# One core, two chained transformer blocks: a k-step of the modulation product as four quarters of 256 columns on TensorE's four column groups, in place of two halves of 512 on two of them

## The chip, the core and the metric

The kernel runs on one core of a Trainium2 chip. The metric is the device time of one execution in microseconds (us); of several runs the median is taken. All data is float32.

## What is computed

A first block of two layers (gated linear attention and latent attention side by side, then an MLP) is followed by a second block of one layer (dilated attention and a long convolution). Each of the three layers is steered by a modulation, a product of one conditioning row with a wide matrix, whose result is cut into shifts, scales and gates:

```python
cond = jax.nn.silu(c)
for l in range(DEPTH):                                   # two layers
    mod = (cond @ w_ada[l] + b_ada[l])[:, None, :]       # 1024 -> 6 x 1024
    shift_a, scale_a, gate_a, shift_f, scale_f, gate_f = jnp.split(mod, N_MOD, axis=-1)
    h = rms_norm(x) * (1.0 + scale_a) + shift_a
    mix = hybrid_mixer(h, ...)
    x = x + gate_a * mix
    h = rms_norm(x) * (1.0 + scale_f) + shift_f
    x = x + gate_f * (jnp.square(jax.nn.relu(h @ w_mlp_up[l])) @ w_mlp_down[l])
...
mod = (c @ w_ada + b_ada)[:, None, :]                    # second block: 1024 -> 3 x 1024
shift, scale, gate = jnp.split(mod, 3, axis=-1)
```

## The kernel before

There are 15 sections of 1,024 modulation values: six for each layer of the first block, three for the second block. `modulation` (L258) computes one section in eight k-steps, one for each 128 rows of the matrix. A k-step loads a tile `wada` of 128 rows by 1,024 columns (512 KB, L270, from SP's queue) and multiplies it with the conditioning column of these rows, which is repeated 32 times (`crep`, L301), so that the product is 32 equal rows. That uses 32 of the 128 columns of TensorE's array, so the product can be put on one of four column groups of 32 (`tile_position`), and products on different groups can run side by side. Two halves `g` of 512 columns stand on two groups, and the k-steps with even and odd `k` use different pairs:

```python
for g in range(2):
    q = 32 * (2 * (k % 2) + g)
    self.mm(ps[q : q + 32], cond[:, k, :], w[:, g * 512 : g * 512 + 512], k < 2, k >= NF - 2, tile_position=(0, q))
yield
```

So the four groups of the accumulator `modps` hold two partial sums of each half, which are added at the end of the section. VectorE copies `modps` into `modrow` (L276). Then the row has to be turned into a column layout (`mod`, 128 by 8). The two sections that the program starts with (`first`) do it on TensorE with products by `pick` (L283 to L286). The other 13 write the row to memory, read it back in column order (L288 to L291, ACT's queue) and add the two partial sums and the bias on VectorE (L292, L293).

The two first sections run in the program's first 50 us. The other 13 run as filling work inside the latent attention (MLA) of the two layers: six sections (48 k-steps) in layer 0, seven (56 k-steps) in layer 1. In `layer1` (L493) the function `spread` asks the generator `fill` for the next k-step twice in each step `n` of the attention loop, in proportion. The final order on each engine is set by a scheduler when the program is built; in the fill a k-step mostly stands alone between products of the attention: scores (`s_ps`), transposes (`tp`), values (`pv`), preparations of the next head (`n_ps`, `mv_ps`, `ms`). A `wada` tile of the fill has three buffers, and `modps` one.

A float32 product such as `modps` shows as two records (two passes) in the trace; the attention's products are of a type that shows as one.

Of the kernel before, what the change touches and what calls it, by code (L numbers as in the profile page):

```python
# [9 lines left out]
F32 = mybir.dt.float32  # L10
# [9 lines left out]
NF = D // 128  # L20
# [141 lines left out]
class Kernel:  # L162
    def __init__(self, tc, ins, consts, out):
        self.tc = tc
        self.nc = tc.nc
        self.i = ins
        self.k = consts
        self.out = out
        self.load = [0.0, 0.0]
# [88 lines left out]
    def modulation(self, p, name, secs, bufs=2, first=False):  # L258

        nc = self.nc  # L260
        cond, w_ada, b_ada = self.ada[name]
        for s in secs:

            if first:
                ps = self.PS.tile([128, 512], F32, name="modps", tag="big", bufs=2, padded_shape=[128, 1024])
            else:
                ps = self.PS.tile([128, 512], F32, name="modps", tag="mod", bufs=1)
            for k in range(NF):
                w = p.tile([128, 1024], F32, name="wada", tag="wada", bufs=bufs + (0 if first else 1))
                nc.sync.dma_start(w, w_ada[k * 128 : (k + 1) * 128, s * 1024 : s * 1024 + 1024])  # L270
                for g in range(2):
                    q = 32 * (2 * (k % 2) + g)
                    self.mm(ps[q : q + 32], cond[:, k, :], w[:, g * 512 : g * 512 + 512], k < 2, k >= NF - 2, tile_position=(0, q))
                yield
            row = p.tile([128, 512], F32, name="modrow", tag="modrow", bufs=1)
            nc.vector.tensor_copy(row, ps)  # L276
            out = self.base.tile([128, NF], F32, name=f"mod_{name}{s}")
            col = self.base.tile([128, 3, NF], F32, name="modcol", tag="modcol", bufs=2)
            nc.scalar.dma_start(col[:, 0], b_ada[s * 1024 : s * 1024 + 1024].rearrange("(j p) -> p j", p=128))
            self.mods[name, s] = out  # L280
            if first:

                cps = self.PS.tile([128, 4, 2], F32, name="modcol_ps", tag="sm", bufs=2, padded_shape=[128, 4, 128])  # L283
                for j in range(4):
                    self.mm(cps[:, j], row[:, j * 128 : j * 128 + 128], self.pick, True, True)
                nc.vector.tensor_add(out.rearrange("p (g j) -> p j g", g=2), cps, col[:, 0].rearrange("p (g j) -> p j g", g=2))  # L286
                continue
            rows = self.DR.tile([4, 512], F32, name=f"modrow_{name}{s}")  # L288
            for q in range(4):
                nc.scalar.dma_start(rows[q].unsqueeze(0), row[32 * q : 32 * q + 1, :])  # L290
            nc.scalar.dma_start(col[:, 1:3], rows.rearrange("(b g) (j p) -> p b (g j)", b=2, p=128))  # L291
            nc.vector.tensor_add(out, col[:, 1], col[:, 2])  # L292
            nc.vector.tensor_add(out, out, col[:, 0])  # L293

    def cond_cols(self, c, silu, name):
        nc = self.nc
# [67 lines left out]
    def consts(self):  # L364
        nc, C, k = self.nc, self.C, self.k
        self.ident = C.tile([128, 128], F32, name="ident")
        nc.sync.dma_start(self.ident, k["ident"])
        self.ones_d = C.tile([128, 128], F32, name="ones_d")
        nc.gpsimd.memset(self.ones_d, -1.0 / 1024)

        self.pick = C.tile([128, 2], F32, name="pick")
        nc.gpsimd.memset(self.pick, 0.0)
        for q in range(4):
            nc.gpsimd.memset(self.pick[32 * q : 32 * q + 1, q % 2 : q % 2 + 1], 1.0)
        self.ones_n = C.tile([128, 128], F32, name="ones_n")
        nc.gpsimd.memset(self.ones_n, -1.0 / 128)
        self.ones_q = C.tile([128, 128], F32, name="ones_q")
        nc.gpsimd.memset(self.ones_q, -1.0 / 256)
        self.ones_r = C.tile([128, 128], F32, name="ones_r")
        nc.sync.dma_start(self.ones_r, k["blockones"])  # L380
        self.eps = C.tile([128, 1], F32, name="eps")
        nc.gpsimd.memset(self.eps, EPS)
# [1600 lines left out]
def trace(tc, ins, consts, out):  # L1983
    Kernel(tc, ins, consts, out).build()
# [21 lines left out]
```

## Time and profile before

| | us |
|---|---|
| three runs | 4498.74, 4505.05, 4512.79 |
| median | 4505.05 |
| the profiled execution | 4509.59 |
| its span in the trace | 4507.8 |
| TensorE matmul busy (PE) | 4159.8 (92%) |
| VectorE (DVE), ScalarE (ACT), GpSimd (POOL) busy | 2098.6, 1492.0, 1483.5 |
| mean granted TensorE clock | 0.961 of full speed |

The span is the time between the first and the last instruction of the profiled execution. PE is the row of matmuls and PEld that of weight loads, which run beside them. Matmuls are pipelined and their ends are modelled, so the time that one costs is read from the starts of its neighbours, not from its length. Timeline rows give start and length in us, then engine, line, operation, output<-inputs, shape and count.

### The profile page before, as it was taken

To read this page: it belongs to the slowest core of one execution; us is meant where nothing else is said; L and a number is where in the kernel's file an instruction comes from. 1 tells how busy PE (TensorE), PEld (TensorE's weight loads), DVE (VectorE), ACT (ScalarE), POOL (GpSimd) and SP (SyncE) were. 2 spreads that over 40 slices of the span, in tenths; PEclk is the share of its full clock that TensorE was granted. 3 is DMA by queue.
4 is the path that set the end of the run, shared out by engine and by line. 5 is a ranking of instruction groups with operands and counts; after the bars stand their busy time and mean duration, and the time that the engine had idled before them with its cause. 6 is when DMAs were issued, how large, how long until landed. Compare 5 with 4: busy or idle time off the path is not lost. (4 is left out here: it accounts for less than half of the span.)

```text
span 4507.8 us, 52345 instructions
## 1 busy us (share of the span) xinstructions
PE 4159.8 (92%) x19660; PEld 3217.8 (71%) x19660; DVE 2098.6 (47%) x3804; ACT 1492.0 (33%) x2824; POOL 1483.5 (33%) x1349
## 2 busy tenths in 40 slices
PE   6999888999999899988999999899999999887998
PEld 3775666888887585566788888667777767766777
DVE  6326575323335516576433333653322434577545
ACT  5435345121212524444312211332224444222222
POOL 3322355333332422155433333222230111355342
PEclk8999899999999999989999999999999999998999
DMA  6145434131111126543211111244453232554563
GB/s 193 57 140 146 150 109 126 43 110 47 52 47 52 42 84 197 156 135 117 76 51 48 47 47 43 93 121 115 112 141 89 85 86 61 178 157 152 167 196 112
DMA packets 579696, 471.25 MB, mean 105 GB/s; under 512 B 210728, under 2 KB 473930, under 8 KB 579314
## 3 DMA queue, kind: packets, MB, share of 16 engines
q1 hardware_dynamic: 375514, 367.43, 26.7%
q10 hardware_dynamic: 203192, 92.74, 7.3%
q0 software_dynamic: 736, 7.73, 0.5%
q8 instruction: 155, 2.54, 0.2%
q14 instruction: 99, 0.81, 0.1%
HBM read 364.22 MB, written 107.52 MB: 105 GB/s over the span
## 5 line engine op out<-in xcount | busy, mean ns | idle before, releaser
L214 POOL TENSOR_TENSOR w_lo<-w_raw,w_hi 128x1024 fp32r<-128x1024 f32 (+4 forms) x222 | 410.6, 1850 | 1025.4 <-ACT w_hi L208 968.3
L205 PE MATMUL dn<-act,dn_hi 128*128 128x512 f32 x2048 | 636.4, 392 | 10.1 <-ACT act L208 4.1
L663 DVE SCALAR_TENSOR_TENSOR xa<-dn,mod,xa 128x512 f32<-128x512 f32 x512 | 383.7, 750 | 277.9 <-PE dn L205 276.3
L205 PE MATMUL in<-b2h,w_hi 128*128 128x512 f32 x1152 | 464.7, 403 | 5.6 <-ACT qkv_t L1627 5.6
L205 PE MATMUL in<-b2h,w_lo 128*128 128x512 f32 x1152 | 464.1, 403 | 0.0
L205 PE MATMUL in<-b2l,w_hi 128*128 128x512 f32 x1152 | 462.5, 402 | 0.0
L208 ACT ACTIVATE w_hi<-w_raw 128x1024 fp32r<-128x1024 f32 (+4 forms) x276 | 236.9, 859 | 675.5 <-PE in L205 260.4
L205 PEld LDWEIGHTS dn<-act,dn_hi 128*128 128x128 f32 x2048 | 386.2, 189 | 95.5 <-ACT act L208 5.6
L205 PE MATMUL up<-fh,w_hi 128*128 128x512 f32 x1024 | 405.9, 396 | 0.4 <-DVE relu L633 0.4
L205 PE MATMUL up<-fl,w_hi 128*128 128x512 f32 x1024 | 404.1, 395 | 1.6 <-POOL fl L214 1.2
L205 PE MATMUL up<-fh,w_lo 128*128 128x512 f32 x1024 | 404.8, 395 | 0.0
L205 PE MATMUL dn<-act,dn_lo 128*128 128x512 f32 x1024 | 401.2, 392 | 2.8 <-POOL dn_lo L214 2.8
L633 DVE TENSOR_TENSOR relu<-up,relu 128x512 f32<-128x512 f32 x128 | 88.4, 691 | 604.2 <-ACT relu L632 604.2
L214 POOL TENSOR_TENSOR dn_lo<-dn_raw,dn_hi 128x1024 fp32r<-128x1024 f32 x64 | 152.3, 2400 | 524.7 <-ACT dn_hi L208 524.7
L205 PEld LDWEIGHTS in<-b2h,w_hi 128*128 128x128 f32 x1152 | 223.4, 194 | 57.0 <-issue 8.6
L205 PEld LDWEIGHTS in<-b2l,w_hi 128*128 128x128 f32 x1152 | 223.6, 194 | 49.2 <-issue 5.9
L205 PEld LDWEIGHTS in<-b2h,w_lo 128*128 128x128 f32 x1152 | 222.7, 193 | 50.1 <-issue 6.9
L208 ACT ACTIVATE dn_hi<-dn_raw 128x1024 fp32r<-128x1024 f32 x64 | 64.8, 1054 | 552.7 <-PE dn L205 545.8
L214 POOL TENSOR_TENSOR act<-relu,act 128x512 fp32r<-128x512 f32 x128 | 167.5, 1309 | 188.8 <-ACT act L208 188.6
L205 PEld LDWEIGHTS up<-fl,w_hi 128*128 128x128 f32 x1024 | 192.9, 188 | 48.8 <-POOL fl L214 3.1
L205 PEld LDWEIGHTS up<-fh,w_hi 128*128 128x128 f32 x1024 | 193.1, 189 | 46.2 <-issue 1.4
L205 PEld LDWEIGHTS up<-fh,w_lo 128*128 128x128 f32 x1024 | 193.2, 189 | 44.9 <-issue 1.0
(503 smaller groups left out, 8407.6 us busy)
## 6 DMA issues: line engine op xcount, KB each, us to landing
wada<-in_w_ada SPq DMA_DIRECT2D x120, 512.0 KB
w_raw<-in_w_in SPq DMA_DIRECT2D x102, 512.0 KB
w_raw<-in_w_mlp_up SPq DMA_DIRECT2D x64, 512.0 KB
dn_raw<-in_w_mlp_down SPq DMA_DIRECT2D x64, 512.0 KB
qkv<-qkv_t ACTq DMA_DIRECT2D x72, 256.0 KB
w_raw<-in_w_out SPq DMA_DIRECT2D x64, 256.0 KB
mix<-mix SPq DMA_DIRECT2D x64, 256.0 KB
spectra<-spec ACTq DMA_DIRECT2D x32, 384.0 KB
```

Of the source, the lines that this page charges most:

```text
L205: return self.nc.tensor.matmul(out, lhsT, rhs, start=start, stop=stop, **kw)
L208: self.nc.scalar.activation(hi, x, AF.Copy, **kw)
L214: return eng.tensor_sub(lo, x, hi.bitcast(F32))
L633: nc.vector.tensor_mul(sq, ps, sq)
L663: nc.vector.scalar_tensor_tensor(x[f, hf], ps, gate[:, f : f + 1], x[f, hf], op0=ALU.mult, op1=ALU.add)
```

## The change

A k-step is cut into four quarters of 256 columns, one on each column group, for even and odd `k` alike. The accumulator uses 256 columns, and each group holds one quarter with nothing left to add. `modrow` and the rows in memory are half as long, the readback has one part, and one of two additions (L292, L293 before) goes. At the program's start two `pick` products of four columns take the place of four of two.

```diff
             for k in range(NF):
                 w = p.tile([128, 1024], F32, name="wada", tag="wada", bufs=bufs + (0 if first else 1))
                 nc.sync.dma_start(w, w_ada[k * 128 : (k + 1) * 128, s * 1024 : s * 1024 + 1024])
-                for g in range(2):
-                    q = 32 * (2 * (k % 2) + g)
-                    self.mm(ps[q : q + 32], cond[:, k, :], w[:, g * 512 : g * 512 + 512], k < 2, k >= NF - 2, tile_position=(0, q))
+                for g in range(4):
+                    q = 32 * g
+                    self.mm(ps[q : q + 32, :256], cond[:, k, :], w[:, g * 256 : g * 256 + 256], k == 0, k == NF - 1, tile_position=(0, q))
                 yield
-            row = p.tile([128, 512], F32, name="modrow", tag="modrow", bufs=1)
-            nc.vector.tensor_copy(row, ps)
+            row = p.tile([128, 256], F32, name="modrow", tag="modrow", bufs=1)
+            nc.vector.tensor_copy(row, ps[:, :256])
             out = self.base.tile([128, NF], F32, name=f"mod_{name}{s}")
-            col = self.base.tile([128, 3, NF], F32, name="modcol", tag="modcol", bufs=2)
+            col = self.base.tile([128, 2, NF], F32, name="modcol", tag="modcol", bufs=2)
...
-                cps = self.PS.tile([128, 4, 2], F32, name="modcol_ps", tag="sm", bufs=2, padded_shape=[128, 4, 128])
-                for j in range(4):
+                cps = self.PS.tile([128, 2, 4], F32, name="modcol_ps", tag="sm", bufs=2, padded_shape=[128, 4, 128])
+                for j in range(2):
                     self.mm(cps[:, j], row[:, j * 128 : j * 128 + 128], self.pick, True, True)
-                nc.vector.tensor_add(out.rearrange("p (g j) -> p j g", g=2), cps, col[:, 0].rearrange("p (g j) -> p j g", g=2))
+                nc.vector.tensor_add(out.rearrange("p (q j) -> p j q", j=2), cps, col[:, 0].rearrange("p (q j) -> p j q", j=2))
                 continue
-            rows = self.DR.tile([4, 512], F32, name=f"modrow_{name}{s}")
+            rows = self.DR.tile([4, 256], F32, name=f"modrow_{name}{s}")
             for q in range(4):
                 nc.scalar.dma_start(rows[q].unsqueeze(0), row[32 * q : 32 * q + 1, :])
-            nc.scalar.dma_start(col[:, 1:3], rows.rearrange("(b g) (j p) -> p b (g j)", b=2, p=128))
-            nc.vector.tensor_add(out, col[:, 1], col[:, 2])
-            nc.vector.tensor_add(out, out, col[:, 0])
+            nc.scalar.dma_start(col[:, 1], rows.rearrange("q (j p) -> p (q j)", p=128))
+            nc.vector.tensor_add(out, col[:, 1], col[:, 0])
...
-        self.pick = C.tile([128, 2], F32, name="pick")
+        self.pick = C.tile([128, 4], F32, name="pick")
...
-            nc.gpsimd.memset(self.pick[32 * q : 32 * q + 1, q % 2 : q % 2 + 1], 1.0)
+            nc.gpsimd.memset(self.pick[32 * q : 32 * q + 1, q : q + 1], 1.0)
```

The scheduler orders the program anew, and the order differs in three places: the first 50 us, and the MLA stage of each layer with the start of what follows it. Elsewhere it is the same on every engine.

TensorE at the start of the fill in layer 0, before (x2 are the two halves of a k-step):

```order
L205 MATMUL s_ps<-kpe_lo_590,qpe_985 128x256
L205 MATMUL modps<-wada,crep_84 32x512 x2
L205 MATMUL n_ps<-nq_0_0_583,w_hi 128x512
L205 MATMUL n_ps<-nq_0_1_586,w_hi 128x512
L205 MATMUL n_ps<-nq_0_0_583,w_lo 128x512
L205 MATMUL n_ps<-nq_0_0_584,w_hi 128x512
```

and with the change:

```order
L205 MATMUL s_ps<-kpe_lo_618,qpe_1013 128x256
L205 MATMUL modps<-wada,crep_84 32x256 x4
L205 MATMUL n_ps<-nq_0_0_611,w_hi 128x512
L205 MATMUL n_ps<-nq_0_1_614,w_hi 128x512
L205 MATMUL n_ps<-nq_0_0_611,w_lo 128x512
L205 MATMUL n_ps<-nq_0_0_612,w_hi 128x512
```

Nothing moved here; four products of 256 columns stand where two of 512 stood. Over the whole fill, counted in this order, uninterrupted groups of `modps` products are: before, 45 in layer 0 and 53 in layer 1, all of one to four halves but one of five (layer 0) and one of seven (layer 1); with the change, 52 and 61, all of one to four quarters but one of 12, three of 5 and one of 8 (layer 0) and four of 8, one of 7 and one of 11 (layer 1).

TensorE in layer 1, in the second head, where most k-steps stand close together, before:

```order
L205 MATMUL modps<-wada,crep_84 32x512
L205 MATMUL ms<-m_sq,ones_n 128x512
L205 MATMUL modps<-wada,crep_84 32x512 x7
L205 MATMUL n_ps<-nkv_0_11188,w_hi 128x512
L205 MATMUL n_ps<-nkv_1_11191,w_hi 128x512
L205 MATMUL n_ps<-nkv_0_11188,w_lo 128x512
L1172 MATMUL tp<-ident,prob 128x128 x4
L205 MATMUL modps<-wada,crep_84 32x512 x4
L1172 MATMUL tp<-ident,prob 128x128 x2
```

and with the change:

```order
L205 MATMUL modps<-wada,crep_84 32x256
L205 MATMUL n_ps<-nkv_0_11306,w_hi 128x512
L205 MATMUL n_ps<-nkv_1_11309,w_hi 128x512
L205 MATMUL n_ps<-nkv_0_11306,w_lo 128x512
L205 MATMUL modps<-wada,crep_84 32x256 x11
L1171 MATMUL tp<-ident,prob 128x128 x3
L205 MATMUL ms<-m_sq,ones_n 128x512
L1171 MATMUL tp<-ident,prob 128x128 x3
L205 MATMUL modps<-wada,crep_84 32x256 x8
```

Six k-steps stood here, and five stand here now, with two more a little ahead of them.

TensorE in the first 50 us, before:

```order
L205 MATMUL modps<-wada,crep_84 32x512 x9
L205 MATMUL ms<-nacc,ones_d 128x512 x2
L205 MATMUL modps<-wada,crep_84 32x512 x4
L205 MATMUL modcol_ps<-pick,modrow 128x2 x4
L205 MATMUL modps<-wada,crep_84 32x512 x15
L205 MATMUL modcol_ps<-pick,modrow 128x2 x4
```

and with the change:

```order
L205 MATMUL modps<-wada,crep_84 32x256 x24
L205 MATMUL ms<-nacc,ones_d 128x512
L205 MATMUL modps<-wada,crep_84 32x256 x7
L205 MATMUL ms<-nacc,ones_d 128x512
L205 MATMUL modcol_ps<-pick,modrow 128x4 x2
L205 MATMUL modps<-wada,crep_84 32x256 x28
L205 MATMUL modcol_ps<-pick,modrow 128x4 x2
```

More of the first section stands ahead of the norm's `ms`, and the `pick` products are half as many.

## Rows read from the trace of the kernel before

**Rows 1.** The page: span, and busy time by engine.

```profile
span 4507.8 us, 52345 instructions
PE 4159.8 (92%) x19660; PEld 3217.8 (71%) x19660; DVE 2098.6 (47%) x3804; ACT 1492.0 (33%) x2824; POOL 1483.5 (33%) x1349
```

**Rows 2.** Busy by engine in the two fills: PE, PEld, DVE, ACT, POOL, PEclk, DMA share, GB/s.

```profile
285.00:485.00 200.00, 188.23 (x952) 114.83 (x950) 121.37 (x287) 96.65 (x208) 46.29 (x72) 0.98 0.53 156
1690.00:1890.00 200.00, 186.63 (x930) 107.84 (x929) 119.27 (x284) 95.12 (x202) 42.48 (x61) 0.97 0.59 176
```

**Rows 3.** Waits of PE in the same windows: us in total, times, longest.

```profile
PE modps L205 <- DMA wada<-in_w_ada: 3.2, 3, 2.0
...
PE modps L205 <- DVE modrow L276: 1.2, 2, 0.8
...
PE modps L205 <- DMA wada<-in_w_ada: 9.0, 4, 3.2
```

**Rows 4.** Groups of instructions, PE, the same windows: busy and mean, idle before.

```profile
L205 PE MATMUL modps<-wada,crep 128*32 128x512 f32 x192 | 52.7, 609 | 4.4 <-DMA wada<-in_w_ada 3.2 <-DVE modrow L276 1.2
...
L205 PE MATMUL modps<-wada,crep 128*32 128x512 f32 x224 | 58.3, 612 | 9.0 <-DMA wada<-in_w_ada 9.0
```

**Rows 5.** Timeline of PE from 292.85 us: one k-step alone.

```profile
292.85 0.28 PE L205 MATMUL s_ps<-kpe_lo,qpe 128*128 128x256 f32 x1
293.06 1.05 PE L205 MATMUL modps<-wada,crep 128*32 128x512 f32 x4
294.05 0.73 PE L205 MATMUL n_ps<-nq,w_hi 128*128 128x512 f32 x2
```

**Rows 6.** Timeline of PE from 326.84 us: two k-steps in one group.

```profile
326.84 1.06 PE L205 MATMUL modps<-wada,crep 128*32 128x512 f32 x8
327.84 0.39 PE L205 MATMUL s_ps<-kn_hi,qn_hi 128*128 128x256 f32 x1
```

**Rows 7.** Timeline of PE from 308.84 us: products of 512 and of 256 columns.

```profile
308.84 0.40 PE L205 MATMUL s_ps<-kpe_hi,qpe 128*128 128x512 f32 x1
309.07 0.40 PE L205 MATMUL s_ps<-kpe_lo,qpe 128*128 128x512 f32 x1
309.31 0.28 PE L205 MATMUL s_ps<-kn_hi,qn_hi 128*128 128x256 f32 x1
309.43 0.27 PE L205 MATMUL s_ps<-kn_lo,qn_hi 128*128 128x256 f32 x1
```

**Rows 8.** Timeline of weight loads (PEld) in a long group at the start.

```profile
27.31 0.13 PEld L205 LDWEIGHTS modps<-wada,crep 128*32 128x32 f32 x4 [0.30 <-issue]
27.74 0.13 PEld L205 LDWEIGHTS modps<-wada,crep 128*32 128x32 f32 x4 [0.30 <-issue]
28.17 0.11 PEld L205 LDWEIGHTS modps<-wada,crep 128*32 128x32 f32 x1 [0.30 <-DMA wada<-in_w_ada]
```

**Rows 9.** Timeline of PE in layer 1's cluster, and a window's busy row after a wait.

```profile
1785.08 1.90 PE L205 MATMUL modps<-wada,crep 128*32 128x512 f32 x10
1790.20 1.28 PE L205 MATMUL modps<-wada,crep 128*32 128x512 f32 x4 [3.22 <-DMA wada<-in_w_ada]
...
441.00:450.00 9.00, 7.90 (x28) 5.04 (x29) 4.41 (x7) 1.23 (x2) 0.00 (x0) 0.62 0.34 113
```

**Rows 10.** Waits of SP's queue in the two fills, the longest of each.

```profile
SPq L270 <- PE modps L205: 125.2, 36, 17.8
...
SPq L270 <- PE modps L205: 124.0, 41, 16.0
```

**Rows 11.** Timeline at the start, PE and DVE: the two first sections.

```profile
42.72 3.63 PE L205 MATMUL modps<-wada,crep 128*32 128x512 f32 x30
48.14 1.05 PE L205 MATMUL modcol_ps<-pick,modrow 128*128 128x2 f32 x8 [1.79 <-DVE modrow L276]
49.23 0.17 DVE L286 TENSOR_TENSOR mod<-modcol_ps,modcol 128x8 f32<-128x8 f32 x1 [1.15 <-PE modcol_ps L205]
```

**Rows 12.** The tile modps: VectorE's copy, ns min/median/max.

```profile
L276 DVE COPY modrow<-modps x15: 673/685/692, 41.0 to 1890.3; 128x512 f32<-128x512 f32 x15
```

## The prediction

> **What bounds the kernel now.** I read the page first: TensorE is busy for 92% of the span and no other engine for half of it [rows 1]. So a change to TensorE's work can move the time, if TensorE is also the bound where that work stands. For that I looked at the two stretches in which the fill runs, 285 to 485 us and 1690 to 1890 us. In each, PE is busy for 188.23 and 186.63 of 200 us, while VectorE is busy for some 120 and ScalarE for 96 [rows 2]. PE idles there for only 11.8 and 13.4 us, and the waits of PE show where: the longest total is that of `modps` itself for its `wada` load, 3.2 and 9.0 us, and 1.2 us for the copy of `modps` to `modrow` [rows 3]. All else is behind PE. What leaves PE here should leave the time.
>
> Then how much of PE is modulation: 192 and 224 records with 52.7 and 58.3 us busy [rows 4], over a quarter of either stretch. These are 48 and 56 k-steps of two halves of two passes.
>
> Last, what a k-step costs. Alone, its four records start at 293.06 and the next product at 294.05, so 0.99 us [rows 5]. Two k-steps in one group, eight records, take from 326.84 to 327.84, so 1.00 us [rows 6]. The second k-step was free: it used the two column groups that the first left empty. That is the place of the change. In a long group, four weight loads come every 0.43 us (27.31 to 27.74) [rows 8], which is then the time of one pass of 512 float32 columns on up to four groups at once. A group of one to four halves is two such passes, 0.86 us, and 0.13 us of emptying behind it. Ahead of it there is a little more: `modps` starts 0.21 us after the last score product [rows 5], where such products of 256 columns follow each other in 0.12 [rows 7]. So I count 0.22 us for each uninterrupted group and 0.86 us for each round of up to four halves.
>
> **The change, part by part.** *The products of the fill.* A quarter has 256 columns. Starts of score products are 0.23 us apart with 512 columns and 0.12 with 256 [rows 7]: the time goes with the columns and leaves no fixed part that could be read, so a pass of a quarter is taken as 0.215 us and a round of up to four quarters, two passes, as 0.43. The groups are counted in the order of instructions.
>
> - Before: layer 0 has 45 groups with 46 rounds, 46 × 0.86 + 45 × 0.22 = 49.5 us; layer 1 has 53 with 54 rounds, 46.4 + 11.7 = 58.1. Together 107.6 us (the busy times of rows 4 are of that size).
> - After: layer 0 has 52 groups with 58 rounds (12 quarters are three rounds, 5 and 8 are two), 58 × 0.43 + 52 × 0.22 = 36.4 us; layer 1 has 61 with 68 rounds, 29.2 + 13.4 = 42.7. Together 79.1 us.
>
> The gain is 28.5 us. The bound on the bad side is that a quarter's pass takes as long as a half's: 126 rounds of 0.86 and 113 × 0.22, 133.2 us, 25.6 more than now. On the good side the count stays 28.5; more than the halved columns cannot go. I take 28.5, since rows 7 show halving directly.
>
> A k-step now has eight passes in place of four. The price of four more is bounded by rows 5 and 6: eight records took 0.01 us longer than four, so 104 k-steps pay 1 us, which I leave within the rounding. The Trainium skill (TensorEngine Tiling (Array Packing), Instruction Overhead) gives each matmul an overhead of about 60 cycles; as an estimate from that page, 416 more passes of 60 cycles at 2.4 GHz, 25 ns, are 10.4 us, and the gain would be 18.1. Rows 6 and 7 don't show such a cost.
>
> *Waits for the loads.* The 104 loads of 512 KB stay, from the same queue with three buffers. SP waits for `modps` to release a buffer for 125.2 and 124.0 us [rows 10], so loads start when a buffer is free; the DMA engines are busy for 0.53 and 0.59 [rows 2], and a stretch shorter by 14 us needs 7% more, so the rate is no bound. What counts are clusters, in which k-steps follow faster than buffers come back. In layer 1 a group of seven halves and the next ran out of buffers: ten records from 1785.08, then 3.22 us of wait until 1790.20 [rows 9]. The new order has a cluster of five k-steps at the same place and one of four in layer 0. PE comes to each fourth load earlier, by about 0.4 us for each k-step before it, so about 1.3 us more wait in each of the two: 3 us, between 6 less (half of today's 12.2 us of waits, where k-steps have moved apart) and 12 more (the waits again).
>
> After a wait the clock falls: in the 9 us from 441 the granted clock was 0.62 on average [rows 9], so three quarters of that stretch, 6.8 us, at 1.2 GHz in place of 2.4, 3.4 us lost. One fall more or less is in the range.
>
> *The copy and the column layout.* VectorE's 13 copies in the fill, 0.685 us each [rows 12], halve at most, and 13 small additions go: some 6 us of an engine with 80 us free in each stretch, hidden behind PE. PE waited for that copy for 1.2 us [rows 3], of which perhaps half goes. The DMAs on ACT's queue stay as many, with half the bytes. Nothing on the path.
>
> *The start.* The second section ends a chain: products from 42.72, copy, `pick` products from 48.14 to the sum at 49.23, on which the first norm waits [rows 11]. The long groups there already fill all four column groups, so the products stay as they are. Half the `pick` records, about 0.5 us of 1.05, and half the copy, 0.3, go from the path. The moved `ms` may add or take a little more. I take 1 us, between 0 and 3.
>
> *The sum.* 28.5 + 1 − 3 = 26.5 us from 4509.6 is 4483 for an execution like the profiled one. That one is 4.5 us over the median of the runs, 4505, so against the median the forecast is **4479 us**.
>
> **The rivals.**
>
> *Waits take the freed time (0.15).* PE no longer is what the stage waits for: loads, the copy, or the chain of scores, exponent and transposes set the pace. For it: `wada` is already the longest wait. Against it: 25 us idle of 400 [rows 2], with VectorE and ScalarE far from full. If half of 28.5 returns as waits, the time is 4505 − 15 = 4490; such cases lie from 4484 to 4500.
>
> *Each pass has a price of its own (0.06).* If passes of a quarter don't quite halve, as in the cited page's rule, 10 us are lost: 4489. Against it speak rows 6.
>
> *Weight loads come out of hiding: slower (0.05).* A k-step has eight loads of 32 columns in place of four, and the passes that hide them are half as long. Four loads take 0.13 us [rows 8]; the point that decides is whether that stays under a pass's 0.215. If loads of a round ran one after another ahead of the passes, at 0.11 us each (the single load at 28.17 there), a k-step would cost 2 × (0.44 + 0.215) = 1.31 us, and 104 of them with 113 × 0.22 would be 161 us, 53 more than now: 4558. The Trainium skill (TensorE: Matmul & The Clock Gate, Part 3, The mechanism) has weight loads overlap running matmuls only where the row group differs, and column groups share theirs, which would be this case. The trace disagrees: in rows 8 the next four loads come while passes run, and passes follow each other every 0.43 us without a gap.
>
> *Quarters run only two at a time (0.04).* Then 104 k-steps at 0.86 and 113 groups are 114 us, 7 more than now: 4512, no change. Rows 6 speak against it.
>
> **How the numbers follow.** The forecast has 0.70: PE stays the bound, and the fill's products halve, with 16 to 38 us gained, so 4467 to 4489. A measurement of this kernel can tell about 0.3% (13.5 us) from no change, so faster means below 4491.5. Nearly all of the first case, half of the second and most of the third give faster: 0.69 + 0.07 + 0.04 = 0.80. Same takes the rest of these and the fourth rival, 0.15. Slower is the load case, 0.05. The range from 4464 to 4500 holds the first three cases but for their edges, and leaves out the last two.
>
> **What would show it.** In the new trace: a k-step alone taking about 0.56 us from its first record to the next product (0.99 before), eight records in it; `modps` busy in the two stretches near 35 and 41 us (0.62 for each group and 0.43 for each further round); the same work of each MLA stage ending about 13 and 15 us sooner relative to its start; PE's waits for `wada` still below 16 us in all; and the stages between, whose order is unchanged, as long as before. It would be wrong if a k-step alone still took 0.9 us or more, if PE's idle time in either stretch rose by over 8 us, or if the gain of the stages were lost behind them.

## The result and the profile after

| | before | after |
|---|---|---|
| median of the runs, us | 4508.92 (4 runs, 4498.74 to 4514.49) | 4469.76 (4 runs, 4464.24 to 4475.41) |
| ratio | | 0.9908 (95%: 0.9888 to 0.9927) |
| the profiled execution, us | 4509.59 | 4475.41 |
| its span, us | 4507.8 | 4473.6 |

The change is faster by 39 us, 0.9%. The forecast was 26.5 us, and 4469.76 lies in its range, toward the fast end.

The page of the changed kernel, span and busy time by engine, against [rows 1]:

```profile
span 4473.6 us, 53257 instructions
PE 4130.8 (92%) x20132; PEld 3220.5 (72%) x20132; DVE 2082.0 (47%) x3791; ACT 1488.5 (33%) x2822; POOL 1488.1 (33%) x1349
```

PE lost 29.0 us of busy time while it gained 472 records, and the span fell by 34.2 us. So most of the gain, 29.0 of 34.2 us, is busy time that left TensorE.

**One k-step.** The timeline of the changed kernel at its first lone k-step, PE and the weight loads (PEld), against [rows 5]:

```profile
287.90 0.28 PE L205 MATMUL s_ps<-kpe_lo,qpe 128*128 128x256 f32 x1
288.11 0.16 PEld L205 LDWEIGHTS modps<-wada,crep 128*32 128x32 f32 x8
288.11 0.64 PE L205 MATMUL modps<-wada,crep 128*32 128x256 f32 x8
288.68 0.72 PE L205 MATMUL n_ps<-nq,w_hi 128*128 128x512 f32 x2
```

Eight records in place of four, and from 288.11 to the next product at 288.68 it is 0.57 us, where it was 0.99. The eight weight loads together are a row of 0.16 us, which lies wholly beside the products.

**The two fills.** From here on I cut every trace at the same marks, so that a stage is measured by itself: the last `qk_ps` product of a layer, its last `s_ps` product (between them lies the fill), and the first `up` product (the MLP). Busy time by engine in the fill and in the stretch behind it, layer 0 and then layer 1; columns as in [rows 2]. Before:

```profile
290.61:483.76 193.15, 181.56 (x920) 109.47 (x919) 120.57 (x286) 96.05 (x207) 45.52 (x70) 0.98 0.55 160
483.76:739.88 256.12, 210.73 (x1029) 163.29 (x1028) 178.80 (x440) 119.03 (x272) 133.36 (x242) 0.91 0.42 132
1689.61:1893.15 203.54, 190.17 (x952) 110.92 (x951) 120.73 (x288) 95.73 (x204) 44.05 (x65) 0.97 0.58 173
1893.15:2152.85 259.70, 217.42 (x1030) 169.21 (x1028) 181.33 (x441) 120.10 (x275) 132.41 (x243) 0.89 0.43 131
```

After:

```profile
285.66:461.90 176.24, 165.54 (x1113) 110.20 (x1111) 116.29 (x282) 96.58 (x207) 46.54 (x70) 0.99 0.58 174
461.90:711.06 249.16, 208.42 (x1029) 161.15 (x1028) 178.45 (x439) 119.14 (x272) 133.56 (x242) 0.93 0.43 136
1659.67:1845.64 185.97, 175.95 (x1176) 114.71 (x1175) 114.94 (x282) 95.37 (x206) 44.91 (x66) 0.96 0.62 191
1845.64:2102.42 256.78, 214.64 (x1029) 165.00 (x1028) 179.96 (x440) 119.23 (x274) 132.43 (x241) 0.90 0.43 131
```

In each fill PE's busy time falls by most of what the stretch loses: by 16.0 of 16.9 us in layer 0 and by 14.2 of 17.6 in layer 1. PE's idle time did not rise (11.6 to 10.7 us, 13.4 to 10.0). So what left PE left the time. The groups of `modps` records and PE's waits in the two fills, against [rows 3, 4]:

```profile
L205 PE MATMUL modps<-wada,crep 128*32 128x256 f32 x384 | 36.2, 392 | 4.9 <-DMA wada<-in_w_ada 4.2 <-DVE modrow L276 0.7
...
L205 PE MATMUL modps<-wada,crep 128*32 128x256 f32 x448 | 43.2, 399 | 6.4 <-DMA wada<-in_w_ada 6.4
```

The products' busy time fell from 52.7 and 58.3 to 36.2 and 43.2 us. The waits for `wada`, which I had expected to grow from 12.2 to some 15 us, are 4.2 + 6.4 = 10.6.

**All stages.** Two executions of each kernel were profiled (the second ones are runs of the first experiment, below). Lengths in us between the marks:

| stretch | before, two | after, two | difference of means |
|---|---|---|---|
| start to the last `qk_ps` of layer 0 | 290.6, 290.9 | 285.7, 288.4 | −3.7 |
| fill, layer 0 | 193.2, 191.0 | 176.2, 179.6 | −14.2 |
| behind it, to the first `up` | 256.1, 258.4 | 249.2, 253.0 | −6.2 |
| to the last `qk_ps` of layer 1 | 949.7, 946.6 | 948.6, 950.2 | +1.3 |
| fill, layer 1 | 203.5, 203.8 | 186.0, 183.3 | −19.0 |
| behind it, to the first `up` | 259.7, 259.1 | 256.8, 253.6 | −4.2 |
| to the end | 2355.0, 2351.0 | 2371.2, 2364.1 | +14.7 |

The fills give 33.2 us, where the forecast had 25.5 (28.5 for the products, less 3 for waits). Two lines were in no term of the forecast: 10.4 us from the two stretches behind the fills, and 14.7 us lost in a last stretch whose order of instructions the change does not touch. The experiments take these apart.

### The profile page after: what moved, and what is told of

It reads as the page before. It is cut to its first block, busy times and chain, and to the rows that moved or that the text cites. A ratio compares the mean times of both kernels' runs of the same rounds, so it can differ in the third digit from the quotient of the medians.

```text
span 4473.6 us, 53257 instructions
## 1 busy us (share of the span) xinstructions
PE 4130.8 (92%) x20132; PEld 3220.5 (72%) x20132; DVE 2082.0 (47%) x3791; ACT 1488.5 (33%) x2822; POOL 1488.1 (33%) x1349
## 5 line engine op out<-in xcount | busy, mean ns | idle before, releaser
L208 ACT ACTIVATE w_hi<-w_raw 128x1024 fp32r<-128x1024 f32 (+4 forms) x276 | 236.8, 859 | 683.1 <-PE in L205 249.2
```

The lines of the kernel that those rows point to most:

```text
L208: self.nc.scalar.activation(hi, x, AF.Copy, **kw)
```

## The experiments

Every kernel computes all of the result. The kernel before and the changed one were run again beside the first two variants.

**1. Both kernels again, and the parts alone.** `before_again` and `after_again` are the two kernels as they are. `fill_only` has the quarters in the 13 sections of the fill alone, `start_only` in the two sections of the first 50 us alone; the other sections keep the code of before:

```diff
+            quarters = not first          # fill_only;  start_only: quarters = first
...
+                if quarters:
+                    for g in range(4):
+                        q = 32 * g
+                        self.mm(ps[q : q + 32, :256], cond[:, k, :], w[:, g * 256 : g * 256 + 256], k == 0, k == NF - 1, tile_position=(0, q))
+                else:
+                    for g in range(2):
+                        q = 32 * (2 * (k % 2) + g)
+                        self.mm(ps[q : q + 32], cond[:, k, :], w[:, g * 512 : g * 512 + 512], k < 2, k >= NF - 2, tile_position=(0, q))
```

> The kernel before, once more, for a second trace. If the 17 us that the second block lost between the two first traces belong to the run and not to the change, this trace's second block (from the first in product to the end) differs from the first trace's by several us at an unchanged order. If they belong to the change, it repeats the first trace's within 2 us. Time 4500 to 4515 either way.

> The changed kernel, once more. Theory: 0.991 of before, 36 to 42 us less; the two attention stages again about 24 and 21 us shorter than before up to the MLPs that follow, the start 5 us, and the second block within 10 us of before on either side. Rival, that part of the stages' gain was luck of the clock in one execution: the stages are 16 and 14 us shorter here.

> Quarters in the 104 k-steps of the fill, halves in the 16 of the start; the order of each part is that of the kernel it is from. Theory: the start's part is 5 us of the gain, so 0.992 to 0.993, 31 to 37 us less than before, with products of modps shorter by 33 us. Rival, that the start counts for nothing at the end: as the full change, 0.991.

> Quarters in the 16 k-steps of the start, halves in the fill. Theory: the first norm's products start 3.5 us earlier and the attention 5 us earlier, and all of it stays: 0.9989, 5 us less. Rival, that it is taken up by a later wait: no change, 1.000.

| | ratio to before (95%) | median, us |
|---|---|---|
| before_again | 1.0001 (0.9988 to 1.0013) | 4509.89 |
| after_again | 0.9903 (0.9882 to 0.9924) | 4470.31 |
| fill_only | 0.9902 (0.9885 to 0.9919) | 4467.50 |
| start_only | 0.9996 (0.9983 to 1.0009) | 4512.59 |

(The runs of before that these share have a median of 4511.87.)

The two repeats confirm the time of the change, and only part of what was expected of its stages. From the last `qk_ps` to the first `up`, the two layers are 23.9 and 20.5 us shorter in the first pair of traces, 16.8 and 25.9 in the second: together 44.4 and 42.7, but divided otherwise. The second block, from the first `in` product to the end, took 1622.2 and 1617.7 us before and 1638.2 and 1630.6 after. So executions of one kernel differ by 4.5 and 7.6 us there, and the expected "within 10 us" missed: 12.9 us remain between the second traces. The account of the last stretch below comes back to this.

The fill's part is, as far as the timing can tell, the whole gain: `fill_only` has the time of the change. Its expectation (0.992 to 0.993) missed, and its rival came. The start alone gives 2 us with an uncertainty of 6, which fits the 5 us of the expectation as well as its rival, no change. In the trace of the changed kernel the start does end earlier. The timeline of its second section, against [rows 11]:

```profile
41.12 3.23 PE L205 MATMUL modps<-wada,crep 128*32 128x256 f32 x56
45.04 0.61 PE L205 MATMUL modcol_ps<-pick,modrow 128*128 128x4 f32 x4 [0.69 <-DVE modrow L276]
45.69 0.17 DVE L286 TENSOR_TENSOR mod<-modcol_ps,modcol 128x8 f32<-128x8 f32 x1 [0.70 <-PE modcol_ps L205]
```

VectorE's sum comes at 45.69 in place of 49.23, but the timed runs cannot tell a gain of that size from none.

**2. Is it four groups or 256 columns?** `split_halves` is the kernel before with each half cut into two products of 256 columns, both on the half's own group. It has the change's eight records of 256 columns in each k-step, and still two groups:

```diff
-                for g in range(2):
-                    q = 32 * (2 * (k % 2) + g)
-                    self.mm(ps[q : q + 32], cond[:, k, :], w[:, g * 512 : g * 512 + 512], k < 2, k >= NF - 2, tile_position=(0, q))
+                for c in (0, 256):
+                    for g in range(2):
+                        q = 32 * (2 * (k % 2) + g)
+                        self.mm(ps[q : q + 32, c : c + 256], cond[:, k, :], w[:, g * 512 + c : g * 512 + c + 256],
+                                k < 2 and c == 0, k >= NF - 2 and c > 0, tile_position=(0, q))
```

> The kernel before, with each half issued as two products of 256 columns on the half's own column group: as many and as small products as the change, on two groups for a k-step. After the last score product, layer 1 then has TensorE's order of the change, layer 0 one of its own. Theory, that time goes with rounds (passes one after another on a group) and groups of products: a k-step alone takes 0.99 us as before; the fill has 105 and 125 rounds of pairs at 0.43 and 52 and 63 groups at 0.22, at most 56.6 and 67.6 us, so up to 7 and 9 us more than before; layer 1 after its last score product is some 6 us shorter, as in the change, if that part is the order's. In all 0 to 16 us slower, 1.000 to 1.0035. Rival, that smaller products as such or the new order make the gain: the fill of modps falls by over 10 us and the kernel is faster by over 0.3%. Rival, a price for each pass of 25 ns: 10 us on top, over 1.0035.

Measured: 0.9985 (0.9969 to 1.0001), 4506.97 us, just under the expected range, with an interval that reaches into it. The timeline of PE at a lone k-step:

```profile
303.52 1.06 PE L205 MATMUL modps<-wada,crep 128*32 128x256 f32 x8
304.50 0.50 PE L205 MATMUL s_ps<-kn_hi,qn_hi 128*128 128x512 f32 x1
```

Eight records of 256 columns on two groups take 0.98 us, on four groups 0.57. The work and the number of records are the same; what the change gains is the two groups that stood empty. Over both fills the time from the first `modps` record of an uninterrupted group to the next other product sums to 115.4 us, with before 113.9 and 113.6 in its two traces, with the change 80.9 and 80.6. So neither smaller products as such nor a new order in the fill makes the gain. This also shows the rival in which quarters run two at a time: a lone k-step would have looked like this one.

**3. What the parity was worth.** `two_groups` is the change with halves in place of quarters: all k-steps, even and odd, use the same two groups. So nothing is to be added at the end either, and only half of the rows are copied and written:

```diff
-                for g in range(4):
+                for g in range(2):
                     q = 32 * g
-                    self.mm(ps[q : q + 32, :256], cond[:, k, :], w[:, g * 256 : g * 256 + 256], k == 0, k == NF - 1, tile_position=(0, q))
+                    self.mm(ps[q : q + 32], cond[:, k, :], w[:, g * 512 : g * 512 + 512], k == 0, k == NF - 1, tile_position=(0, q))
...
```

(The dots stand for the copy, the rows and `pick`, which take the shape of two halves.)

> The kernel before with both k-parities on the same two column groups, so that two k-steps never run side by side. After the last score product, layer 0 has TensorE's order of the change. Theory of rounds: the fill has 63 and 68 rounds of 0.86 us and 59 and 66 groups of 0.22, 67 and 73 us for 49.5 and 58.1 of the kernel before, 33 us more; the start's 17 rounds for 9 cost up to 7 more; layer 0 after its last score product is some 7 us shorter, if that part is the order's. In all 20 to 40 us slower, 1.0045 to 1.009. Rival, that column groups give nothing and a long group's speed comes from elsewhere: within 0.3% of before.

Measured: 0.9994 (0.9980 to 1.0008), 4506.64 us. The expectation missed. Its mechanism is there: two k-steps in one group no longer share their time. The timeline of PE:

```profile
438.40 1.91 PE L205 MATMUL modps<-wada,crep 128*32 128x512 f32 x8
440.25 1.12 PE L205 MATMUL ms<-m_sq,ones_n 128*128 128x512 f32 x2
```

1.85 us, where the kernel before takes 1.00 for the same eight records [rows 6]. Over both fills the groups' time, measured as for `split_halves`, sums to 131.7 us, 17.8 more than before's 113.9. But the two fills together grew by only 7.7 against the means of before, and the stretches behind them shrank by 15.4. Its windows, fill and stretch behind it in layer 0, then the fill of layer 1:

```profile
289.34:483.98 194.64, 192.54 (x920) 110.20 (x919) 118.32 (x283) 98.31 (x207) 47.23 (x70) 1.00 0.52 157
483.98:734.38 250.40, 208.18 (x1030) 160.99 (x1028) 178.20 (x439) 119.16 (x272) 133.69 (x242) 0.93 0.43 136
...
1681.07:1889.85 208.78, 201.98 (x952) 111.56 (x951) 119.98 (x282) 96.10 (x206) 44.31 (x66) 0.99 0.58 171
```

With slower products the loads keep up: PE waits for `wada` for 0.3 and 4.3 us in the two fills, and it idles for 2.1 and 6.8 us. The granted clock is 1.00 and 0.99 there, where it was 0.98 and 0.97. (An estimate: a mean of 0.98 over 193 us is 7.7 us at the lower of the two levels, which is half the speed, so 3.9 us lost; the two fills together get back about 8, or 6 against the second trace of before, with 0.99 and 0.97.) I had priced the slower products, and neither the waits that they remove nor the order behind the fill.

That order is the other finding here. In layer 0, `two_groups` has on TensorE, behind the fill, the same order as the change, and with halves in the fill this stretch takes 250.4 us, as with the change (249.2 and 253.0), against 256.1 and 258.4 before. `split_halves` has the change's order behind the fill of layer 1 alone, and there it takes 253.6 us, as with the change (256.8 and 253.6), against 259.7 and 259.1; in layer 0, with an order of its own, 256.6. The window of `split_halves` behind the fill of layer 1:

```profile
1894.14:2147.72 253.58, 210.57 (x1029) 162.51 (x1028) 179.27 (x441) 119.35 (x274) 133.03 (x241) 0.91 0.45 132
```

The other traces agree. With the change's order the stretch takes 248.4 to 253.0 us in layer 0 (five traces) and 250.6 to 256.8 in layer 1 (five traces), with the order of before 255.6 to 258.4 and 259.1 to 260.7 (three traces each); kernels with halves and with quarters in the fill are on the faster side of both. So the 10 us do not need quarters. They go with the order that the scheduler made when the fill's costs changed. On TensorE behind the fill of layer 0, before (`D`, `sufk` and `A` are the linear attention, `wo` the output product):

```order
L205 MATMUL D<-levels,la_hi_4213 128x512
L205 MATMUL D<-levels,la_lo_4214 128x512
L205 MATMUL wo<-mix,w_hi 128x512
L205 MATMUL sufk<-la_hi_4213,suffix 128x128
L205 MATMUL sufk<-la_lo_4214,suffix 128x128
L205 MATMUL wo<-mix,w_hi 128x512
L205 MATMUL wo<-mix,w_lo 128x512
L205 MATMUL sufk<-la_hi_4213,suffix 128x128
```

and with the change:

```order
L205 MATMUL D<-levels,la_hi_4331 128x512
L205 MATMUL D<-levels,la_lo_4332 128x512
L205 MATMUL wo<-mix,w_hi 128x512 x2
L205 MATMUL wo<-mix,w_lo 128x512
L205 MATMUL wo<-mix,w_hi 128x512 x2
L205 MATMUL wo<-mix,w_lo 128x512
L205 MATMUL sufk<-la_hi_4331,suffix 128x128
L205 MATMUL wo<-mix,w_hi 128x512
```

Two full sets of `wo` products now stand together ahead of `sufk`. PE's waits there, before:

```profile
PE wo L205 <- DVE xa L615: 9.4, 5, 2.5
...
PE wo L205 <- DMA mix<-mix: 6.2, 2, 4.1
...
PE tp L1172 <- DVE mo L1188: 3.0, 1, 3.0
```

and after:

```profile
PE wo L205 <- DVE xa L614: 7.6, 5, 2.3
...
PE wo L205 <- DVE chunk_decay L922: 2.3, 1, 2.3
```

The wait of 3.0 us for `mo` is no longer among the longer ones, that for `xa` is shorter by 1.8, and the granted clock of the stretch rose from 0.91 to 0.93. These three repeat in the second traces; the 6.2 us for `mix` do not: there they are 2.5 before and 2.2 after. Which of these small waits earned which microsecond was not tested.

**4. A fourth buffer, and k-steps in pairs.** A k-step alone pays the emptying of TensorE each time: 104 k-steps stand in 113 groups. `four_buffers` is the change with one more `wada` buffer in the fill. `pairs` has that buffer, and asks for two k-steps at a time, half as often. `pairs_three_buffers` is `pairs` without the buffer; `pairs_of_halves` is the kernel before (halves, three buffers) with pairs. Of the three cuts below, the first is the buffer and the other two are the pairs:

```diff
-                w = p.tile([128, 1024], F32, name="wada", tag="wada", bufs=bufs + (0 if first else 1))
+                w = p.tile([128, 1024], F32, name="wada", tag="wada", bufs=bufs + (0 if first else 2))
...
-                yield
+                if k % 2:
+                    yield
...
-            steps = 8 * sum(len(secs) for _, secs in mods)
+            steps = 4 * sum(len(secs) for _, secs in mods)
```

> The change with four buffers of wada in the fill in place of three. Theory: TensorE's waits for wada, 4.2 and 6.4 us in the change's first trace, fall below 4 us together, and with them a fall or two of the clock; 5 to 12 us less than the change, 0.988 to 0.990 of before. Rival, that the loads' rate and not the buffers make the waits: they stay above 8 us and the time stays at 0.9905.

> The change with four buffers, and the fill handing out k-steps two at a time. The order has 41 and 41 groups of modps products for 52 and 61, at as many rounds (62 and 65). Theory: 31 groups less at 0.22 us are 7 us, with the waits for wada as with four buffers: 7 us less than that kernel, about 0.987 of before. Rival, that pairs take two buffers at a time and wait for loads again: as the four buffers alone or slower.

> The change with the fill handing out k-steps two at a time, but three buffers as in the change. The order has 40 and 44 groups and 57 and 66 rounds of 0.43 us, 71 us for 79 of the change. Theory: 8 us less than the change by the count, less what pairs lose by waiting for loads with three buffers, some 4 to 10 us: 0.989 to 0.991, no better than the change, and the fourth buffer is what lets pairs gain. Rival, that the fourth buffer does nothing also with pairs: 0.9875, as pairs with four.

> The kernel before, with the fill handing out k-steps two at a time (three buffers as before): an even and an odd k-step together fill the four column groups without quarters. TensorE's order breaks the pairs into 42 and 45 groups with 43 and 47 rounds of 0.86 us, 96.5 us with 0.22 a group, for 107.6 before; after the last score product both layers have the order that layer 1 has with the change. Theory: 11 us from the fill and 12 from what follows it, 15 to 28 us less, 0.994 to 0.9965. Rival, that pairs do all that quarters do: 0.990 or less. Rival, that the order after the fill gives nothing by itself: 0.9975.

| | ratio to before (95%) | median, us |
|---|---|---|
| four_buffers | 0.9906 (0.9887 to 0.9925) | 4467.32 |
| pairs | 0.9874 (0.9853 to 0.9895) | 4453.11 |
| pairs_three_buffers | 0.9913 (0.9897 to 0.9928) | 4471.76 |
| pairs_of_halves | 0.9932 (0.9915 to 0.9948) | 4481.50 |

`four_buffers` missed: its time is that of the change, and the waits for `wada` in its two fills are neither below 4 us, as expected, nor above 8, as its rival had it. PE's waits there:

```profile
PE modps L205 <- DMA wada<-in_w_ada: 3.3, 5, 1.5
...
PE modps L205 <- DMA wada<-in_w_ada: 3.7, 3, 2.9
```

7.0 us in place of 10.6, worth less than the timing can tell. `pairs` is the fastest kernel of all here, 1.26% under before, as expected, and some 13 us under the change by the ratios (0.9874 against 0.9903). A pair of k-steps, in the timeline of PE:

```profile
309.81 1.07 PE L205 MATMUL modps<-wada,crep 128*32 128x256 f32 x16
310.81 0.66 PE L1172 MATMUL tp<-ident,prob 128*128 128x128 f32 x4
```

16 records take 1.00 us, so two k-steps pay the emptying once (two lone ones are 2 × 0.57 = 1.14, and the time ahead of each). PE's waits for `wada` in its two fills:

```profile
PE modps L205 <- DMA wada<-in_w_ada: 1.6, 3, 0.7
...
PE modps L205 <- DMA wada<-in_w_ada: 4.9, 6, 1.4
```

By the timed runs neither part does it alone: the buffer without pairs gives nothing that shows, and pairs with three buffers have the time of the change, just over the expected range. A pair takes two buffers at once, and with three only one is left to load ahead. PE's waits for `wada` in the fills of `pairs_three_buffers` are indeed twice those of `pairs`:

```profile
PE modps L205 <- DMA wada<-in_w_ada: 5.1, 5, 1.6
...
PE modps L205 <- DMA wada<-in_w_ada: 7.9, 8, 2.4
```

But the two fills hardly tell the difference. They take 353.2 us with `pairs` and 355.5 with `pairs_three_buffers`, against 362.6 with the change, so the pairs shorten the fills with three buffers too, by 7.1 us for 8 counted. Of the 16.9 us that `pairs_three_buffers` takes longer than `pairs` between the two traces, 2.2 lie in the fills, 6.6 behind them and 8.0 in the other stretches, of which the long ones have the same order on TensorE. So that the fourth buffer is what lets pairs gain is not shown.

`pairs_of_halves` says how much of the change was there to be had without quarters: with three buffers, pairing lets two halves fill the groups that one k-step leaves empty, and gains 30 us. Quarters with pairs and three buffers gain 40. The 30 us lie just over the expected 15 to 28, and they come from other parts than expected. Its windows, fill and stretch behind it, layer 0 and then layer 1:

```profile
289.86:476.67 186.81, 177.55 (x921) 109.72 (x920) 120.53 (x287) 96.91 (x207) 46.41 (x70) 0.98 0.56 165
476.67:732.94 256.27, 213.79 (x1029) 166.24 (x1028) 178.39 (x440) 118.62 (x272) 133.21 (x242) 0.90 0.42 132
1682.53:1870.94 188.41, 180.18 (x953) 108.24 (x951) 121.23 (x290) 95.98 (x206) 45.38 (x70) 0.99 0.63 189
1870.94:2126.58 255.64, 214.47 (x1030) 165.87 (x1029) 178.65 (x439) 118.96 (x273) 132.85 (x241) 0.89 0.44 131
```

Against the means of before the fills are 20.5 us shorter, for 11 expected, and the stretches behind them 4.7, for 12. In layer 0 the order that goes with a gain in layer 1 gave next to nothing (256.3 us, before 256.1 and 258.4). That the sum came near was luck.

## Why the prediction was right

The decision, the sign and the bound were right: TensorE bounds the fill, and the groups that stood empty were the cost. The forecast of 26.5 us came out low against the measured 39. In the traces the change gains 46 us ahead of the last stretch: 10.4 are a term that was missing, and the fills give 7.7 and the start 2.7 more than forecast. The last stretch takes 14.7 back in these traces. By its steps:

- **The products of the fill (28.5 us).** Right, and near in size. Lone k-steps take 0.57 us (0.56 was forecast). `modps` is busy for 36.2 and 43.2 us (35 and 41 were said), 31.6 less than before, and the groups' time fell by 33.0, from 113.9 to 80.9. By the prediction's count, 0.86 or 0.43 us for each round and 0.13 us for each group, these would be 98.7 and 68.9, a fall of 29.8; what is left over belongs to the next step. The fills are 14.2 and 19.0 us shorter, for 13 and 15 said. In `split_halves`, the passes of 256 columns save nothing as long as they run on two groups.
- **The waits for the loads (+3 us).** The sign was wrong. Beyond the count, the `modps` groups hold 15.2 us before and 12.0 after, in which waits and time at the lower clock lie: −3.2 us. I reasoned that PE comes to each fourth load of a cluster earlier. I left out that the new order moves k-steps apart elsewhere, which I had named for the low end of that term only; no run tests whether this is the reason. The wait for `wada` went from 12.2 to 10.6 us in the first pair of traces, and from 11.5 to 10.1 in the second.
- **The start (1 us less, between 0 and 3).** The traces show 3.7 less, and the timed runs of `start_only` 2 with an uncertainty of 6. The size stays open.
- **The copy and the column layout (nothing).** Right. The copy takes 417 ns in place of 685 [rows 12], and PE's wait for it went from 1.2 to 0.7 us. The tile `modps` of the changed kernel:

```profile
L276 DVE COPY modrow<-modps x15: 410/417/425, 38.5 to 1841.8; 128x256 f32<-128x256 f32 x15
```

- **The step that is missing.** The prediction has no term for the stretches behind the fills. The orders differ there too, as the section on the change says, and I took their cost as unchanged. They give 10.4 us, which `two_groups` and `split_halves` show to go with the new order, not with the quarters. That the measurement still lies in the range is owed to the range's width and not to this step.
- **The stretches between** are as long as before (+1.3 us), as said. **The last stretch** is longer by 14.7 us in the profiled executions, with the same order. Its windows in the two traces that lie furthest apart, before (the second execution) and after (the first):

```profile
2149.70:4500.70 2351.00, 2188.43 (x10417) 1731.24 (x10415) 1032.85 (x1747) 684.78 (x1309) 708.62 (x472) 0.97 0.35 104
```

```profile
2102.42:4473.60 2371.18, 2204.01 (x10417) 1738.83 (x10415) 1029.97 (x1746) 684.81 (x1309) 712.28 (x472) 0.96 0.35 103
```

The same 10,417 matmuls are busy for 15.6 us longer, at a lower granted clock. Over all twelve traces this stretch, with the same order on TensorE, takes 2351 to 2371 us. The two executions of before are the lowest of them, and the first one of the change is the highest. Quarters in the fill are not what lengthens it: four other kernels with halves there (`start_only`, `split_halves`, `two_groups`, `pairs_of_halves`) take 2359.9 to 2364.5 us, and the six traces with quarters 2356.7 to 2371.2. I take it mostly as variation between executions: without it the stages sum to −46 us, with it to −31, and the timed runs say −39 and −42. Why the two traces of before are lowest, and whether a few of these microseconds are the change's, stays open.

Of the rivals, none came. Idle time in the two fills together fell, from 25.0 to 20.7 us and in the second traces from 24.2 to 22.1, though in layer 0 alone it rose there by 2.0. A pass of a quarter has no price of its own that shows (eight records in 0.57 us, sixteen in 1.00), the loads stayed hidden, and the quarters run four at a time. The Trainium skill (TensorEngine Tiling (Array Packing), Instruction Overhead) would have had the products gain 18.1 us, by the estimate in the prediction; the fill's `modps` records are busy for 31.6 us less, so the trace disagrees here with that price as time added for each pass. The Trainium skill's rule that weight loads overlap running matmuls only where the row group differs (TensorE: Matmul & The Clock Gate, Part 3, The mechanism) does not hold here either: the eight loads of a k-step lie beside its products.

## What to carry to other kernels

When small products stand alone between others, look at how much of the array one of them leaves empty, and cut it so that it fills the array by itself; a partner that would fill the rest seldom stands beside it once a scheduler has spread the work. Then try the pieces in larger groups, with the buffers that a larger group holds at once: here the two together gained another 13 us, and neither gained alone in the timed runs. And where a scheduler rebuilds the order, count the stretches behind the change as a term of their own, with both signs in the range, and compare them with another kernel that has the same order there.

## What was not expected of the hardware

- Eight weight loads of 32 columns on four column groups are a row of 0.16 us beside the products; four took 0.13 [rows 8]. Here twice as many loads cost no time that shows.
- A slower product seems to have got part of its price back by the clock (6 to 8 us by the estimate above): in the fills of `two_groups`, with PE idle for only 2.1 and 6.8 us, the granted clock was 1.00 and 0.99, against 0.98 and 0.97 before, with 11.6 and 13.4 us idle. It is no strict rule here: with the change, idle times of 10.7 and 10.0 us go with 0.99 and 0.96.
- The same order on TensorE takes from 2351 to 2371 us in the last stretch over twelve traces, and the two executions of one kernel differ there by 4.0 us (before) and 7.1 (after). A difference of that size between two single traces says little there.
